# Reordering sixteen matmuls around a late transpose, and dropping four matmuls on zeros, at the start of a 4096 x 4096 matmul with bias and tanh

## Chip, cores, metric

One core of one Trainium2 chip. The metric is device microseconds of one execution. The profile's span (first to last instruction) is about 1.7 us shorter than that.

## The reference

```python
def reference(a, b, bias):          # all 4096 x 4096 float32, bias 4096
    return np.tanh(np.matmul(a, b) + bias)
```

## The kernel before

The product runs in fp16: TensorE multiplies a 128x128 block of A, transposed, by a 128x512 block of B. B is taken in four column chunks of 1024 (J = 2 halves of 512), A in row tiles of 128 rows, and the sum over 4096 runs over 32 k-tiles. One matmul is one row tile, one k-tile, one half.

The first chunk starts before anything is loaded, so it is done in a special order. Groups 0 and 1 of four row tiles each (G = 4) take turns over the k-tiles as they arrive: group 0 over 1 to 4, group 1 over 1 to 8, group 0 over 5 to 16, group 1 over 9 to 32. The part sums of a pass are put aside in SBUF ("spill") and added again later. Eight 128x512 sums (4 row tiles x 2 halves) of a group take all eight PSUM buffers ("banks" below) of the kernel's pool, so a group can only start when sums of the other have been moved out.

```python
def across(ps, ms, t0, t1, first):          # k-tile by k-tile, over the row tiles ms
    for t in range(t0, t1):
        for m in ms:
            for j in range(J):
                mm(ps[m][j], ats[m], b_cur, t, j, t == first, False)

def down(ps, ms, t0, t1, done):             # closes the sums one after the other
    for m in ms:
        for j in range(J):
            for t in range(t0, t1):
                mm(ps[m][j], ats[m], b_cur, t, j, False, t == t1 - 1)
            done(ps[m][j], m, j)            # here add_aside: spill += ps on VectorE

def fill(n, w):                             # n matmuls of w columns on zeros
    ...

# the first row tiles, turned on TensorE, with zeros between them (lines joined here)
turn_nat(0, nc.vector.tensor_copy); fill(3, P); turn_nat(1, nc.scalar.copy)
row(0, 0, 2); fill(2, P); turn_nat(2, nc.vector.tensor_copy)
row(1, 0, 2); fill(2, P); turn_nat(3, nc.scalar.copy)
row(2, 0, 2); row(3, 0, 2)
across(ps, g0, 2, BL - 1, 0)
...
# the order of the loads, all on one queue (KS = 8, KM = 16, BL = TB = 4):
want_a("g0b", G, 0, G * Q, BL, BL)                 # group 0's A, k-tiles 5..8
want_a("g0c", G, 0, G * Q, KS, KM - KS)            # group 0's A, k-tiles 9..16
for u in range(KS, KM, 2):
    want(lambda u=u: load_b_all(u, 2))             # B in pairs, four quarters each
want_a("g1c", ...); want_a("g1d", ...)             # group 1's A, k-tiles 9..16
...                                                # the bias
for t in (KM, KM + 8):
    want_a(("g1", t), G, 4 * P, G * Q, t, 8)
    for u in range(t, t + 8, TB):
        want(lambda u=u: load_b_all(u, TB))        # B four k-tiles at a time
...
# the passage that is reordered
for m in g0:
    turn(ats[m], "g0c", m * Q, KS, KM - KS)        # VectorE transposes
one_by_one(ps, g0, BL, KS, BL)                     # k-tiles 5..8
across(ps, g0, KS, KM - 1, BL)                     # k-tiles 9..15
for i in range(2):
    turn(ats[G + i], "g1c", i * Q, KS, KM - KS)
down(ps, g0, KM - 1, KM, add_aside)                # k-tile 16, frees the banks
...
one_by_one(ps, g1, KS, KM, KS)                     # group 1, k-tiles 9..16
for t in (KM, KM + 8): ...                         # group 1, k-tiles 17..28
```

## Time and profile before

| | |
|---|---|
| device time, 3 runs | 1782.67 us median, 1782.46 to 1783.02 |
| span of the profile | 1780.8 us |
| TensorE | busy 100% of the span, 8258 matmuls |
| its idle time before instructions, whole span | 2.3 us in three waits |

The profile's lines are in the prediction. In a timeline the first two numbers are the start and the length in us, then engine, source line, operation, tiles written and read, and how many instructions were merged; the bracket gives the idle time ahead of them and what ended it. Lengths of matmul groups overlap, so starts are what to compare. The landing of a transfer is its issue time plus the last column of the DMA issues.

### The profile page before, as it was taken

How to read it: one execution, taken by the hardware profiler on the slowest of the kernel's cores; microseconds unless marked ns; L12 is line 12 of the kernel's file. 1: busy time of each engine (PE TensorE's matmuls, PEld its weight loads, DVE VectorE, ACT ScalarE, POOL GpSimd, SP SyncE). 2: the span in 40 equal slices, each digit the busy share in tenths (PEclk: the TensorE clock that was granted, in tenths of full speed). 3: DMA queues.
4: the chain of work that ended last, by engine and by line, in shares of the span. 5: the costliest groups of instructions: out<-in, count | busy, mean ns of one | idle time of the engine just before them, and what ended most of it. 6: DMA issues, size and time to landing. Idle time of an engine off the chain costs nothing.

```text
span 1780.8 us, 20862 instructions
## 1 busy us (share of the span) xinstructions
PE 1775.0 (100%) x8258; PEld 807.1 (45%) x8258; DVE 764.1 (43%) x680; ACT 173.0 (10%) x279; POOL 872.0 (49%) x1618
## 2 busy tenths in 40 slices
PE   9999999999999999999999999999999999999999
PEld 4444444444444444444444444444444444444444
DVE  3764443444334443444334443444344443444342
ACT  2021000000000000000000000000000000000001
POOL 7565566544565554444456554444544454444510
PEclk9999999999999999999999999999999999999999
DMA  9999999976999877767699987766777667766641
GB/s 185 204 194 177 176 167 154 140 125 110 167 173 165 145 112 116 118 116 120 113 170 171 172 136 116 118 116 108 128 116 122 107 113 117 120 114 109 117 77 42
DMA packets 281393, 238.94 MB, mean 134 GB/s; under 512 B 159056, under 2 KB 231760, under 8 KB 281296
## 3 DMA queue, kind: packets, MB, share of 16 engines
q0 software_dynamic: 243280, 167.88, 69.8%
q1 hardware_dynamic: 37728, 69.62, 11.0%
q8 instruction: 64, 1.05, 0.2%
q14 instruction: 33, 0.27, 0.1%
q10 hardware_dynamic: 288, 0.13, 0.0%
HBM read 337.64 MB, written 67.11 MB: 227 GB/s over the span
## 4 chain that ended last, share of the span: by engine, by line
PE 97%; DMA 1%; POOL 0%; DVE 0%; issue 0%; ACT 0%; DVEq 0%; POOLq 0%
PE ps L412 93%; PE ps L138 5%; DMA b<-in_b_dram 1%; DMA an<-in_a_dram 0%; DVE atx L100 0%; POOL an L90 0%; POOL nat L246 0%; POOL b L69 0%; ACT o_sb L152 0%; DVE o_sb L149 0%; POOL ident L263 0%; POOLq L263 0%; DVEq L100 0%; DVEq L149 0%; POOLq L435 0%
## 5 line engine op out<-in xcount | busy, mean ns | idle before, releaser
L412 PE MATMUL ps<-b,at 128*128 128x512 f16 x7712 | 1657.8, 378 | 0.0
L90 POOL DMA_DIRECT2D an<-in_a_dram x1492 | 805.4, 547 | 797.4 <-DVE at L100 592.0
L412 PEld LDWEIGHTS <-at 128*128 128x128 f16 x7712 | 754.6, 98 | 903.3
L100 DVE STREAM_TRANSPOSE at<-an 128x512 f16<-128x512 f16 (+1 forms) x380 | 565.5, 1539 | 65.8 <-DMA an<-in_a_dram 65.8
L149 DVE TENSOR_TENSOR o_sb<-ps,bias_bc 128x512 f32<-128x512 f32 (+1 forms) x243 | 165.7, 683 | 918.4 <-PE ps L412 710.3
L152 ACT ACTIVATE o_sb<-o_sb 128x512 f32<-128x512 f32 (+1 forms) x243 | 151.6, 625 | 1502.3 <-DVE o_sb L149 1502.3
L73 POOL DMA_DIRECT2D b<-in_b_dram x104 | 56.2, 544 | 15.3 <-DMA an<-in_a_dram 7.8
L138 PE MATMUL ps<-b,atx 128*128 128x512 f16 x256 | 56.4, 379 | 0.5 <-DVE atx L100 0.5
L138 PE MATMUL ps<-b,at 128*128 128x512 f16 x256 | 55.6, 379 | 0.0
L138 PEld LDWEIGHTS <-at 128*128 128x128 f16 x256 | 25.0, 98 | 30.2
L138 PEld LDWEIGHTS <-atx 128*128 128x128 f16 x256 | 24.6, 98 | 30.7 <-DVE atx L100 1.8
L100 DVE STREAM_TRANSPOSE atx<-an 128x512 f16<-128x512 f16 (+2 forms) x12 | 16.3, 1399 | 12.3 <-DMA an<-in_a_dram 12.3
L69 POOL DMA_DIRECT2D b<-in_b_dram x12 | 7.8, 654 | 22.5 <-PE ps L412 22.3
L152 ACT ACTIVATE spill<-spill 128x512 f32<-128x512 f32 x16 | 9.9, 630 | 82.9 <-DVE spill L149 82.9
L149 DVE TENSOR_TENSOR spill<-ps,spill 128x512 f32<-128x512 f32 x16 | 10.4, 679 | 10.1 <-PE ps L138 10.1
L181 DVE TENSOR_TENSOR spill<-spill,bias_bc 128x512 f32<-128x512 f32 x16 | 9.7, 677 | 0.0
L173 ACT COPY spill<-ps 128x512 f32<-128x512 f32 x16 | 8.0, 623 | 12.9 <-PE ps L138 12.9
L228 PE MATMUL ps<-zeros 128*128 128x512 f16 (+1 forms) x18 | 5.6, 463 | 1.3 <-DVE zeros L221 1.3
L176 DVE TENSOR_TENSOR spill<-ps,spill 128x512 f32<-128x512 f32 x8 | 4.8, 672 | 0.0
L228 PEld LDWEIGHTS <-zeros 128*128 128x128 f16 x18 | 2.1, 126 | 4.2 <-issue 2.5
L239 DVE CAST b<-spill 128x1024 f16<-128x1024 f32 x1 | 0.9, 871 | 4.5 <-DMA spill<-in_b_dram 4.5
L246 POOL DMA_DIRECT2D nat<-in_a_dram x4 | 2.3, 586 | 0.8 <-POOLq L435 0.8
(14 smaller groups left out, 8.8 us busy)
## 6 DMA issues: line engine op xcount, KB each, us to landing
an<-in_a_dram POOLq DMA_DIRECT2D x480, 192.0 KB, 5.1
out_dram<-o_sb SPq DMA_DIRECT2D x239, 256.0 KB, 2.5
an<-in_a_dram POOLq DMA_DIRECT2D x960, 32.0 KB, 2.6
b<-in_b_dram POOLq DMA_DIRECT2D x94, 256.0 KB, 8.0
b<-in_b_dram POOLq DMA_DIRECT2D x6, 1024.0 KB, 13.2
an<-in_a_dram POOLq DMA_DIRECT2D x32, 128.0 KB, 5.6
out_dram<-spill SPq DMA_DIRECT2D x16, 256.0 KB, 5.6
an<-in_a_dram POOLq DMA_DIRECT2D x12, 256.0 KB, 8.3
```

What stands on the lines that cost most here:

```text
L69: queue.dma_start(out=dst, in_=src[:, ds(t0 % BL, nt), :])
L73: nc.gpsimd.dma_start(out=bt[t0 // TB][ds(q * QP, QP), ds(t0 % TB, nt), :], in_=src.rearrange("(t p) n -> p t n", p=QP),)
L90: nc.gpsimd.dma_start(out=an[ds(q * QP, QP), :, ds((t - t0) * QP, n * QP)], in_=src.rearrange("(mb p) k -> p mb k", p=QP),)
L100: nc.vector.transpose(at[:, ds(t, n), :].rearrange("P t (mb p) -> P mb t p", p=QP), an[:, ds(mb0, Q), ds((t - t0) * QP, n * QP)].rearrange ...
L138: nc.tensor.matmul(ps, at[:, t, :], bt[t // TB][:, t % TB, ts(j, NB)], start=start, stop=stop)
L149: nc.vector.tensor_tensor(out=o_sb[:, piece], in0=ps[:, piece], in1=addend[:, piece], op=mybir.AluOpType.add)
L152: nc.scalar.activation(o_sb[:, piece], o_sb[:, piece], mybir.ActivationFunctionType.Tanh)
L173: nc.scalar.copy(aside(m, j), ps)
L176: nc.vector.tensor_tensor(out=aside(m, j), in0=ps, in1=aside(m, j), op=mybir.AluOpType.add)
L181: nc.vector.tensor_tensor(out=aside(m, j), in0=aside(m, j), in1=bias_bc[:, ts(j, NB)], op=mybir.AluOpType.add)
L228: nc.tensor.matmul(ps[:, ds(0, w)], zeros[:, :P], zeros[:, :w], start=i == 0, stop=i == n - 1)
L412: nc.tensor.matmul(ps, at[:, t, :], b_cur[t // TB][:, t % TB, ds(c0, w)], start=t == 0, stop=t == KT - 1,)
```

## The change

Intent: the k-tiles 9 and 10 were run across all four row tiles, so TensorE stood still until the fourth row tile had been turned. With both k-tiles of a row tile together there are four matmuls to do for each row tile, not two, while the next is being turned. The zeros between the first rows are dropped, as they fill no wait.

```diff
     row(0, 0, 2)
-    fill(2, P)
     turn_nat(2, nc.vector.tensor_copy)
     row(1, 0, 2)
-    fill(2, P)
     turn_nat(3, nc.scalar.copy)
 ...
     one_by_one(ps, g0, BL, KS, BL)
-    across(ps, g0, KS, KM - 1, BL)
+    for m in g0:
+        across(ps, (m,), KS, KS + 2, BL)
+    across(ps, g0, KS + 2, KM - 1, BL)
```

## The prediction

> **What bounds the kernel now.** I read the page first: busy time by engine and the chain that ended last. Then the waits of TensorE over the whole span, then the timelines of TensorE, its weight loads and VectorE over the first 51 us, where both edits lie. These lines are the page's:
>
> ```profile
> PE 1775.0 (100%) x8258; PEld 807.1 (45%) x8258; DVE 764.1 (43%) x680; ACT 173.0 (10%) x279; POOL 872.0 (49%) x1618
> ...
> PE 97%; DMA 1%; POOL 0%; DVE 0%; issue 0%; ACT 0%; DVEq 0%; POOLq 0%
> ```
>
> TensorE is the chain. The count is 8258 matmuls: 8192 for the product, 32 more because the last tile is halved, 16 transposes and 18 matmuls on zeros. Only a matmul that disappears from TensorE's queue, or a wait of TensorE that ends sooner, can move the time. The waits view lists all of TensorE's waits:
>
> ```profile
> PE ps L228 <- DVE zeros L221: 1.3, 1, 1.3
> PE ps L138 <- DVE atx L100: 0.5, 1, 0.5
> PE tp L257 <- DMA nat<-in_a_dram: 0.5, 1, 0.5
> ```
>
> One of them, on a VectorE transpose into atx (group 0's A tiles), concerns the change. Next, TensorE's timeline (start, length, count), with the zeros that go away and then the passage that is reordered:
>
> ```profile
> 7.43 1.04 PE L138 MATMUL ps<-b,atx 128*128 128x512 f16 x4
> 8.31 0.28 PE L228 MATMUL ps<-zeros 128*128 128x128 f16 x2
> 8.42 0.39 PE L257 MATMUL tp<-ident,nat 128*128 128x128 f16 x4
> 8.64 1.03 PE L138 MATMUL ps<-b,atx 128*128 128x512 f16 x4
> 9.51 0.28 PE L228 MATMUL ps<-zeros 128*128 128x128 f16 x2
> 9.62 0.39 PE L257 MATMUL tp<-ident,nat 128*128 128x128 f16 x4
> ```
>
> ```profile
> 28.83 8.54 PE L138 MATMUL ps<-b,atx 128*128 128x512 f16 x38
> 37.90 12.69 PE L138 MATMUL ps<-b,atx 128*128 128x512 f16 x58 [0.52 <-DVE atx L100]
> 50.42 41.60 PE L138 MATMUL ps<-b,at 128*128 128x512 f16 x192
> ```
>
> Use the starts, not the lengths, because the ends overlap. From 37.90 to 50.42 there are 58 matmuls, so one takes 0.216 us. By that pace the 38 matmuls from 28.83 would be through at 28.83 + 38 x 0.2158 = 37.03; the next starts at 37.90. So 0.87 us is lost in that stretch, more than the 0.52 that the waits view shows. The weight loads show where:
>
> ```profile
> 35.79 0.56 PEld L138 LDWEIGHTS <-atx 128*128 128x128 f16 x4 [0.38 <-DVE atx L100]
> 36.76 0.11 PEld L138 LDWEIGHTS <-atx 128*128 128x128 f16 x2 [0.41 <-DVE atx L100]
> 37.89 0.55 PEld L138 LDWEIGHTS <-atx 128*128 128x128 f16 x4 [1.01 <-DVE atx L100]
> ```
>
> The load at 35.79 opens the ninth k-tile (32 matmuls after 28.83, due at 35.74); those at 36.76 and 37.89 open its third and fourth row tile. What released each is in VectorE's timeline and in the DMA issues:
>
> ```profile
> 33.22 4.62 DVE L100 STREAM_TRANSPOSE atx<-an 128x1024 f16<-128x1024 f16 x4 [2.89 <-DMA an<-in_a_dram]
> 47.43 2.37 DVE L100 STREAM_TRANSPOSE at<-an 128x1024 f16<-128x1024 f16 x2 [9.59 <-DMA an<-in_a_dram]
> 49.72 2.44 DVE L176 TENSOR_TENSOR spill<-ps,spill 128x512 f32<-128x512 f32 x4
> ```
>
> ```profile
> 28.03 0.54 POOL L73 DMA_DIRECT2D b<-in_b_dram  x1 [0.23 <-DMA an<-in_a_dram]
> ```
>
> ```profile
> b<-in_b_dram POOLq DMA_DIRECT2D x1, 128.0 KB, 7.7
> ```
>
> Four transposes from 33.22 to 37.84, one per row tile, end some 1.13 apart: about 34.46, 35.59, 36.71 and 37.84. The last two match the loads at 36.76 and 37.89. The first stall is different: the releaser view names VectorE, but row tile 0 was turned at 34.46. The last quarter of B's ninth and tenth k-tile, issued at 28.03, landed 7.7 us later, at 35.73. That is the event the load at 35.79 follows. So the 0.87 us is about 0.08 waiting for B and 0.77 waiting for transposes, with 0.02 of pipeline restart.
>
> **What the Trainium skill says.** "TensorE: Matmul & The Clock Gate", section "Wait — 56ns, not 53.3ns?", gives 55.6 and 215.7 ns between warm matmuls of 128 and 512 columns. The trace agrees: two zero matmuls take 8.31 to 8.42, 55 ns each, and a 512-column one 216 ns. The same page, Part 1, has the clock fall after an idle window of about 3.4 us; the trace's longest stall past the warm-up is about 0.7 us and the granted clock stays full, so a moved stall of that size should not cost speed. "PSUM — Partial Sum Buffer", section "The four PSUM rules", says one matmul output takes at most one bank; its specifications list eight banks. This kernel's eight open 128x512 sums of group 0 therefore fill PSUM: group 1's first sum waits for a freed bank. The same page, "Engine vs sequencer instructions", says VectorE's queue is strict FIFO. The trace agrees: the add that empties the first bank starts at 49.72, behind the two transposes that started at 47.43, although the sum it reads ended near 49.08 (matmul start 48.70 plus 0.38).
>
> **The change part by part.**
>
> 1. *Zeros removed.* Four 128-column matmuls at 55.8 ns: TensorE gets 0.22 us ahead from 8.31 on. The transposes that follow need A tiles already loaded (they ran at once, with no wait, in the trace). Each copy of a transposed tile moves with its transpose, and the distance from transpose to the row that uses it is unchanged or is still ample. VectorE's turn of row tile 0 for k-tiles five to eight, which began at 27.83 and takes about 0.71, ends at 28.54, while the shifted matmul is due at 28.61: it just holds.
>
> 2. *But at the ninth k-tile* TensorE now arrives at 35.74 - 0.22 = 35.52, and B still lands at 35.73. Transfers do not depend on TensorE here: their buffers come free through VectorE's transposes, which wait for transfers. So the first matmul stays at 35.82 and the 0.22 is gone.
>
> 3. *Two k-tiles per row tile.* From 35.82 each row tile has 4 matmuls, 0.863 us, in place of 2. Row tile 1 is due at 36.68 (turned 35.59), 2 at 37.55 (36.71), 3 at 38.41 (37.84). The smallest reserve is 0.57. B's tenth k-tile comes in the same transfers as the ninth. The 16 matmuls end at 35.82 + 16 x 0.2158 = 39.27, where before they ended at 37.90 + 10 x 0.2158 = 40.06. Gain: 0.79 us. The three later B pairs are issued from 29.34 on and land 5.3 us later in the median, the first of them complete at 38.20: over a microsecond of reserve.
>
> 4. *What follows.* After k-tiles 11 to 15, the eight closing matmuls shift from 48.70 to 47.91 and TensorE is ready for group 1 at 49.63 in place of 50.42. Its first sum needs the bank of group 0's first sum. VectorE's order is unchanged: two transposes, from 47.43 because their A transfer landed just then, then the add. The transposes hold it until 49.72; the add takes 0.65, so the bank is free at 50.37, and with the 0.05 us that the earlier releases took (37.84 to 37.89) TensorE starts at 50.42. That is exactly where it starts now: in this trace the two paths, the late transposes through 58 matmuls and the transfer through VectorE, meet within 0.01 us. The change shortens one of them.
>
> Sum: 0.22 + 0.79 gained on TensorE, 0.22 given back at 35.8, 0.79 at 50.4. Net 0.0 us. After 50.42 TensorE has no wait to the end, so nothing is gained or lost there.
>
> **The rivals.** (a) *The gain passes through*: time falls by 0.79 to 1781.9. For it: the waits view shows no wait at 50.42. Against it: only because both paths tie; the add's start at 49.72 does not involve TensorE. (b) *The zeros' 0.22 counts also*: 1781.66. Against it: B's landing at 35.73. (c) *The tie was chance*: the transfers of single executions jitter, and in some the transposes' path was the later one, so the change saves the excess. The three times before differ by 0.56 us, so I allow 0.1 us on average. (d) *Slower*: with two zero tiles fewer, PSUM banks are handed out in another order, and a row might wait for a copy. All copies but the last row tile's are done well before, and that row needs its copy anyway: under 0.2 us, 1782.8. (e) *A clock effect* from the missing zeros: transposes take only 0.22 us between rows, so I expect none.
>
> **Range and chances.** From the median 1782.67, with 0.0 by the working and 0.1 for (c): 1782.6. The low end, 1781.8, takes in rival (a) with a little scatter; the high end, 1783.1, is the slowest run before plus 0.1. Two per cent is 36 us, while all of TensorE's waits sum to 2.3 us: within 2% is 0.99, faster 0.004, slower 0.006.
>
> **What would show it right or wrong.** Right: TensorE has 8254 matmuls; no wait on atx; the ninth k-tile still opens at about 35.8 and the weight load's idle time there grows from 0.38 to 0.60; a new TensorE wait appears on the add into spill, of about 0.6 (0.79 less the modelled overlap of 0.16), ending near 50.4; group 1's passage starts within 0.1 of 50.42. Wrong: that passage starting near 49.6, which would mean the bank came free earlier, or VectorE's add not behind the transposes; or the ninth k-tile opening at 35.6, which would mean B is not what holds it. A wait later than 50.4 would also refute it.

## The result

The first four runs of the changed kernel took 1781.87 us in the median (1781.57 to 1782.08), beside 1782.85 for the four of before (1782.46 to 1784.16). The ratio is 0.9993, with an interval of 0.9976 to 1.001. Ratios here are the mean time of one kernel's runs over that of the other's in the same rounds, so not quite the ratio of the medians. The kernel won about 0.8 us by its median against the 1782.67 foretold from, where the prediction had the net at nothing and allowed 0.1.

Single executions scatter with a standard deviation of 0.55 us, so I pool. Over all, before has 45 runs with a mean of 1782.72 us and the changed kernel 14 with 1782.20: 0.52 us less, with a standard error of 0.16 (the root of the sum of the two squared errors). These pools cross chips. They also show that the first four runs were lucky: a gain of 0.52 us on 1782.67 would be 1782.15.

The page of the changed kernel, busy times and the chain:

```profile
PE 1774.4 (100%) x8254; PEld 806.9 (45%) x8254; DVE 763.8 (43%) x680; ACT 173.2 (10%) x279; POOL 872.1 (49%) x1618
...
PE 99%; DMA 0%; issue 0%; ACT 0%; POOL 0%; DVE 0%; DVEq 0%; POOLq 0%
```

Four matmuls fewer, as they should be. TensorE's timeline of the changed kernel:

```profile
8.31 0.39 PE L257 MATMUL tp<-ident,nat 128*128 128x128 f16 x4
...
28.70 21.10 PE L138 MATMUL ps<-b,atx 128*128 128x512 f16 x96
49.63 41.84 PE L138 MATMUL ps<-b,at 128*128 128x512 f16 x192
```

The transpose now follows the row at 8.31, where the zeros stood. All 96 matmuls of group 0 run in one piece, where they were broken at 37.90. Group 1's passage opens at 49.63, not at 50.42: the 0.79 us of step 3 to the hundredth, and no wait on the bank. This is a sign that the prediction had named for being wrong.

The weight loads of the changed kernel, at the ninth and at the 25th k-tile, and VectorE behind group 1's opening:

```profile
35.79 13.51 PEld L138 LDWEIGHTS <-atx 128*128 128x128 f16 x64 [0.51 <-DVE atx L100]
```

```profile
76.83 0.10 PEld L138 LDWEIGHTS <-at 128*128 128x128 f16 x1
77.47 0.13 PEld L138 LDWEIGHTS <-at 128*128 128x128 f16 x2 [0.55 <-DVE spill L181]
```

```profile
46.16 2.37 DVE L100 STREAM_TRANSPOSE at<-an 128x1024 f16<-128x1024 f16 x2 [8.22 <-DMA an<-in_a_dram]
48.46 4.84 DVE L176 TENSOR_TENSOR spill<-ps,spill 128x512 f32<-128x512 f32 x8
```

The ninth k-tile opens at 35.8, as before, after a longer idle time (0.51 for 0.38; 0.60 was predicted). VectorE began its transposes for group 1 at 46.16, not at 47.43, because A's transfer landed sooner; so the add that frees the first bank was done at 49.11, before TensorE came. And there is a new stall: the 25th k-tile opens at 77.50 (the load at 77.47), 0.24 late.

That stall is not in TensorE's waits view, since the modelled end of the matmul before it covers most of it, and the weight loads' view names a bias add on VectorE that had ended at 77.01. The DMA issue of the last quarter of B's k-tiles 25 to 28 tells more. First the issue and its landing time in the changed kernel, then the same in the kernel before:

```profile
66.62 0.55 POOL L73 DMA_DIRECT2D b<-in_b_dram  x1 [0.68 <-DMA b<-in_b_dram]
```

```profile
b<-in_b_dram POOLq DMA_DIRECT2D x1, 256.0 KB, 10.6
```

```profile
67.52 0.55 POOL L73 DMA_DIRECT2D b<-in_b_dram  x1 [0.71 <-DMA b<-in_b_dram]
```

```profile
b<-in_b_dram POOLq DMA_DIRECT2D x1, 256.0 KB, 10.1
```

It landed at 77.26 in the changed kernel and 77.60 in the one before (unrounded). TensorE opened the 25th k-tile at 77.50 and 78.05. "Perfetto Trace Analysis", section "Identifying Dependency Chains", says that an instruction that waits for several engines may have extra semaphore instructions ahead of it. The trace has two here, one behind the other, and with them the 0.24 us from landing to opening; in all four profiles that stall there, the lag is 0.24 or 0.25. So before the change, B held the 25th k-tile to 77.84 at the earliest, and TensorE came 0.21 later. After it, TensorE would have come at 77.26 and B held it. Of the 0.79, 0.55 is left at 77.50, and the spans differ by just that, 1780.8 and 1780.2. From the opening of the 25th k-tile to the end of the span it is 1702.72 us in both, and 1702.71 to 1702.73 in all 17 profiles: what is not won by then is not won at all.

### The profile page after: what moved, and what is told of

Its sections match the earlier page's. It is cut to its first block, busy times and chain, and to the rows that moved or that the text cites. A ratio compares the mean times of both kernels' runs of the same rounds, so it can differ in the third digit from the quotient of the medians.

```text
span 1780.2 us, 20854 instructions
## 1 busy us (share of the span) xinstructions
PE 1774.4 (100%) x8254; PEld 806.9 (45%) x8254; DVE 763.8 (43%) x680; ACT 173.2 (10%) x279; POOL 872.1 (49%) x1618
## 4 chain that ended last, share of the span: by engine, by line
PE 99%; DMA 0%; issue 0%; ACT 0%; POOL 0%; DVE 0%; DVEq 0%; POOLq 0%
PE ps L412 93%; PE ps L138 6%; DMA nat<-in_a_dram 0%; ACT o_sb L152 0%; PE tp L257 0%; POOL nat L246 0%; DVE o_sb L149 0%; DVEq L149 0%; POOLq L435 0%
```

## The experiments

For every profile I read the same four openings. Without a stall, group 1 opens 48 matmuls (10.36 us at 0.2158) after group 0's eleventh k-tile, and the 25th k-tile 128 matmuls (27.62 us) after that. What exceeds these is the wait at group 1's bank and the wait for B:

| kernel | 9th opens | 11th | group 1 | 25th | bank wait | B wait | VectorE starts group 1's transposes | B's last quarter lands |
|---|---|---|---|---|---|---|---|---|
| before | 35.82 | 40.06 | 50.42 | 78.05 | 0 | 0 | 47.43 | 77.60 |
| before, again | 35.95 | 40.03 | 50.39 | 78.02 | 0 | 0 | 46.77 | 77.70 |
| zeros out only | 35.83 | 40.16 | 50.52 | 78.14 | 0 | 0 | 46.74 | 77.79 |
| reordering only | 35.84 | 39.28 | 49.65 | 78.21 | 0 | 0.94 | 46.35 | 77.97 |
| changed | 35.82 | 39.27 | 49.63 | 77.50 | 0 | 0.24 | 46.16 | 77.26 |
| changed, again | 36.77 | 40.22 | 50.60 | 79.02 | 0.02 | 0.79 | 47.60 | 78.77 |
| changed, third | 35.84 | 39.29 | 50.03 | 77.65 | 0.38 | 0 | 47.03 | 77.20 |

My first theory (T1) was that the reordering's 0.79 us passes through because the tie at 50.42 was chance, and that the zeros bring nothing. The rivals were that the zeros carry a share (R1) and my prediction (R2).

### Zeros out only

The two `fill(2, P)` are removed and the old `across` stays.

> Only the four zero matmuls are taken out; the ninth and tenth k-tile stay as before. Theory T1 (the gain is the reordering's; the time won by the zeros is lost again where B's ninth k-tile lands at 35.8 us): time as before, within 0.2 us; group 1's passage starts near 50.4 us. Rival R1 (the zeros carry a share): 0.2 us faster than before. Rival R2 (my prediction: the bank that group 1 needs comes free no sooner than TensorE arrives): as before.

Time: 1782.57 us median, ratio 0.9999 (0.9986 to 1.0011). The weight load that opens the ninth k-tile:

```profile
35.80 0.56 PEld L138 LDWEIGHTS <-atx 128*128 128x128 f16 x4 [0.55 <-DVE atx L100]
```

The ninth k-tile opens as before, after a longer idle time (0.55 for 0.38). In this profile R1 is out: the zeros' 0.22 us ends at B's landing, as step 2 had it. The times cannot tell 0 from 0.2.

### Reordering only

The zeros stay; the passage is that of the change.

> Only the reordering of the ninth and tenth k-tile; the zero matmuls stay. T1: as the whole change, 0.5 to 0.8 us faster than before; group 1's passage starts at 49.6 us with no wait on the add into spill in most profiles. R1: 0.2 us slower than the whole change. R2: the passage starts when the bank is free, as late as 50.4 if A's transfer for group 1 lands at 47.3 as it did before.

Time: 1782.66 us median, 1781.91 to 1784.29; ratio 1.0 (0.9988 to 1.0013). The expected 0.5 to 0.8 us did not show. TensorE's timeline of this kernel:

```profile
49.65 27.79 PE L138 MATMUL ps<-b,at 128*128 128x512 f16 x128
78.21 2.10 PE L138 MATMUL ps<-b,at 128*128 128x512 f16 x9 [0.78 <-DMA b<-in_b_dram]
```

Group 1 opens as early as with the whole change, and then the 25th k-tile waits for B: 0.94 us, more than all that was won. Here the waits view names the transfer itself. T1 is only half right: the bank does let the gain through, and another place takes it.

### Before and changed, a second time

Both unedited.

> The kernel before, unchanged, for a second profile and for the noise. T1: A's transfer for group 1 lands about a microsecond sooner than the 47.3 us of the first profile, so that the tie at 50.42 us was chance; time ratio 1.000 within 0.0002. R2: it lands at 47.3 again and the tie is there again.

> The changed kernel, unchanged, for a second profile. T1: group 1's passage starts at 49.6 us, A's transfer for it lands near 46 us, and the wait of some 0.2 us for B's 25th k-tile at 77.5 us is there again, so that the time is 0.5 to 0.8 us below before. R2: a profile of this kernel in which that transfer lands at 47.3 us shows a wait on the add into spill of up to 0.6 us and a start at 50.4 us.

Before: ratio 0.9999, no tie: VectorE's transposes began at 46.77, 0.66 sooner than in the first profile, while TensorE opened group 1 at 50.39:

```profile
46.77 2.37 DVE L100 STREAM_TRANSPOSE at<-an 128x1024 f16<-128x1024 f16 x2 [8.96 <-DMA an<-in_a_dram]
```

Changed: median 1782.15, ratio 0.9996 (0.9982 to 1.001); its profiled run happened to be the slowest of its five, 1783.46. TensorE's timeline in it:

```profile
29.64 21.10 PE L138 MATMUL ps<-b,atx 128*128 128x512 f16 x96 [0.61 <-ACT spill L173]
50.60 27.79 PE L138 MATMUL ps<-b,at 128*128 128x512 f16 x128
79.02 13.32 PE L138 MATMUL ps<-b,at 128*128 128x512 f16 x61 [0.63 <-DVE spill L181]
```

The whole start is late by 0.95: VectorE's turn for k-tiles 5 to 8 began at 28.87, not at 27.93, behind a later transfer, and the later landings are late too. The releaser that the view names at 29.64 and at 79.02 is not the cause in either place. That led to my second theory, T3: TensorE follows the transfers from 29 us to 79 us, and what it wins between two of them it gives back at the next. It does not hold at every opening: in the second profile of before, B's ninth k-tile landed at 35.61, 0.34 before TensorE opened it. The DMA row of the kernel before, 25 to 50 us in 40 slices, shows the DMA engines busy 90% or more in all slices but one, so the transfers run nearly without a pause:

```profile
DMA  9999999999999999999989999999999999999999
```

### Finer load of B's 25th k-tile, with and without the change

```diff
-        for u in range(t, t + 8, TB):
-            want(lambda u=u: load_b_all(u, TB))
+        for u, nt in ((t, TB), (t + TB, TB)) if t == KM else ((t, 2), (t + 2, 2), (t + TB, TB)):
+            want(lambda u=u, nt=nt: load_b_all(u, nt))
```

> The changed kernel with B's k-tiles 25 to 28 loaded as two pairs in place of four at once, so that the 25th and 26th land some 2.5 us sooner. Theory T3 (what the change won by 49.6 us is partly lost where TensorE opens the 25th k-tile, because B's last quarter for it lands there; the transfers of the first 80 us set that moment): no stall at the 25th k-tile, which opens 27.6 us after group 1's passage started (64 matmuls to the 17th, 64 to the 25th, at 0.2158 us); of the order of 0.2 to 0.9 us faster than the changed kernel, with a smaller spread of the times. Rival R3 (the stall at the 25th k-tile is VectorE's, which the waits view names: its transposes of A or its bias adds): the stall stays and the time is that of the changed kernel.

> The kernel before with the same finer load. T3: before the change TensorE reached the 25th k-tile just after B did, so little is gained: 0 to 0.3 us, and the whole change on top of it is then worth 0.8 us in the opening of the 25th k-tile. R3: as before, and the change is worth no more than without the finer load.

With the change: 1781.93 us median, ratio 0.9996 (0.9983 to 1.001), and the passage of group 1 through the 25th k-tile in one piece:

```profile
49.66 41.60 PE L138 MATMUL ps<-b,at 128*128 128x512 f16 x192
```

B now lands at 74.83, and the 25th k-tile opens at 77.29, 27.63 after the passage began. R3 is out: nothing on VectorE was edited, and the stall is gone in this profile and in the four later ones that have the new order and the finer load. The 0.2 to 0.9 us over the changed kernel, which I expected, did not show in the times (the pools at the end say 0.12 +- 0.18). Without the change: 1782.89, ratio 1.0 (0.9987 to 1.0012), opening at 78.45 because the ninth had opened 0.3 late, at 36.14. The finer load alone is worth nothing, as T3 has it. The expected smaller spread did not come (1781.74 to 1782.86).

### Two useless transposes ahead of the adds

Group 1's second row tile is turned twice more, which holds VectorE 2.25 us longer before the add that frees the first bank. Results stay right.

```diff
+    g1c_an = staged["g1c"][0]
     for i in range(2):
         turn(ats[G + i], "g1c", i * Q, KS, KM - KS)
+        if i == 0:
+            for _ in range(2):
+                transpose_a(ats[G + 1], g1c_an, Q, KS, KM - KS)
```

> The changed kernel with group 1's second row tile turned twice more than needed (2.25 us of VectorE) ahead of the adds that free group 0's banks. This makes the wait that my prediction expected. If the bank path works as predicted and only its time was wrong, TensorE waits 1.5 to 1.9 us at the opening of group 1's passage, released by the add into spill; the 25th k-tile then opens without a stall at 79.0 to 79.4 us and the time is 0.9 to 1.5 us above the changed kernel's. If the bank is not what group 1 waits for, no wait and no change.

> The kernel before with the same two useless turns. If the bank path had a reserve of some 0.6 us in most executions (T1), group 1's passage starts 1.4 to 1.7 us late and the change is worth nothing on top: the passage opens within some tenths of the same moment as in the changed kernel with these turns, the rest being the jitter of the transfers. If the tie of the first profile were the rule (R2), it starts 2.25 us late, at 52.7 us.

One run each: 1783.68 and 1784.54 us. TensorE's timeline with the change, then without:

```profile
51.62 40.74 PE L138 MATMUL ps<-b,at 128*128 128x512 f16 x188 [1.79 <-DVE spill L176]
```

```profile
52.49 39.87 PE L138 MATMUL ps<-b,at 128*128 128x512 f16 x184 [1.05 <-DVE spill L176]
```

So the mechanism that I predicted is real: delay the add, and group 1 waits for it, 1.95 us start to start with the change and 1.22 without. The opening is 5.56 us after VectorE's first transpose in both (46.06 and 46.93). The two openings are 0.87 apart, more than the tenths expected, because the transfers were. With the change the 25th k-tile opened at 79.25 without a stall, as expected. The waits are a little outside what I had written (1.5 to 1.9 and 1.4 to 1.7).

### Group 0's A in two halves around B's ninth k-tile

On top of the finer load, with the zeros out, and then with the zeros put back (the turns of row tiles 3 and 4 then read `g0c2`, not shown):

```diff
-    want_a("g0c", G, 0, G * Q, KS, KM - KS)
-    for u in range(KS, KM, 2):
+    want_a("g0c", 2, 0, 2 * Q, KS, KM - KS)
+    want(lambda: load_b_all(KS, 2))
+    want_a("g0c2", 2, 2 * P, 2 * Q, KS, KM - KS)
+    for u in range(KS + 2, KM, 2):
         want(lambda u=u: load_b_all(u, 2))
```

> The changed kernel with two edits of the order of its loads: B's 25th and 26th k-tile ahead of the 27th and 28th (as in the earlier run), and group 0's A for k-tiles 9 to 16 loaded in two halves, two row tiles before B's ninth and tenth k-tile and two after. T3: B's ninth k-tile then lands near 33 us and the stall at its opening (0.21 us in three profiles of four with the change) is gone; no stall at the 25th. The 25th k-tile opens 0.2 to 0.3 us sooner than with the finer load alone, near 77.05 us when the transfers before 28 us are not late; 0.7 to 1.1 us faster than before. Rival: the split only moves the stall to a transpose of the third or fourth row tile, or to later pairs of B, and nothing is won over the finer load alone.

> The same with the four zero matmuls put back. T3: with B's ninth k-tile no longer holding TensorE, the zeros show for the first time: the ninth k-tile opens 0.1 to 0.22 us later than without them, unless the transposes for k-tiles 5 to 8 hold TensorE at 28.7 us in that run, in which case nothing shows. Rival: no difference in any case, as TensorE waits for something else.

1782.25 us median, 1782.18 to 1782.50, ratio 0.9998 (0.9984 to 1.0011); and one look at 1782.17 with the zeros. B's ninth k-tile lands at 33.20 and the stall at its opening is gone (35.69 without zeros, 35.88 with them: 0.19, within the 0.1 to 0.22 that the zeros were expected to show). But the rival came true. Without the zeros 0.19 us is lost at the fourth row tile of the ninth k-tile, whose A now comes in the later half. Its transpose, the second of the two from 36.04, ended at 38.41, and its weight load follows at 38.47:

```profile
36.04 2.37 DVE L100 STREAM_TRANSPOSE atx<-an 128x1024 f16<-128x1024 f16 x2 [2.89 <-DMA an<-in_a_dram]
38.47 2.06 PEld L138 LDWEIGHTS <-atx 128*128 128x128 f16 x11 [0.52 <-DVE atx L100]
```

B's eleventh k-tile, which also landed at 38.47, was needed only at 39.35. With the zeros, where the ninth opened later, nothing is lost there, and both have the same start of the 11th k-tile to 0.02 us (39.35 and 39.33). Then the bank binds, by 0.46 us without the zeros and 0.42 with them. TensorE without them:

```profile
50.16 41.60 PE L138 MATMUL ps<-b,at 128*128 128x512 f16 x192 [0.29 <-DVE spill L176]
```

The 25th opens at 77.79 without zeros and 77.73 with them. The split wins nothing in its profiles, and the finer load alone does not guarantee the gain: the bank can take it. Its five times lie closest together of all, which I have not followed up.

### Changed, a third time; finer load, a second time

> The changed kernel a third time, beside the others on one chip. T3: 0.3 to 0.9 us faster than before, with a stall of 0.2 to 0.8 us at the 25th k-tile that ends about 0.24 us after the last quarter of B lands.

> The changed kernel with the finer load of B's 25th k-tile, a second time. T3: no stall at the 25th k-tile, which opens 27.6 us after group 1's passage; between the changed kernel and the one with both edits in time, within the scatter of some 0.4 us of each mean.

Changed: 1782.57 us median, ratio 0.9998 (0.9985 to 1.001), and, against the expectation, no stall at the 25th but the bank wait that I had predicted. TensorE and VectorE in it:

```profile
50.03 41.60 PE L138 MATMUL ps<-b,at 128*128 128x512 f16 x192 [0.22 <-DVE spill L176]
```

```profile
47.03 2.37 DVE L100 STREAM_TRANSPOSE at<-an 128x1024 f16<-128x1024 f16 x2 [9.09 <-DMA an<-in_a_dram]
```

The bank comes free 3.00 us after the transposes start: 47.03 to 50.03 here, 47.60 to 50.60 in the second profile, 47.43 to 50.42 in the first of before. It binds where this sum is later than TensorE. Finer load: 1782.05, ratio 0.9997 (0.9984 to 1.0009); transfers late at the ninth (36.54), group 1 at 50.35, the 25th at 77.97, no wait for the bank or for B. The transposes began at 47.35 here, so the bank came free at 50.35 too: a tie once more.

### Both gates opened

There are thus two gates, places where TensorE may have to wait: the bank at group 1's opening and B at the 25th k-tile. The finer load opens the second. The first opens with the adds of row tile 0 put ahead of the second turn on VectorE:

```diff
-    for i in range(2):
-        turn(ats[G + i], "g1c", i * Q, KS, KM - KS)
-    down(ps, g0, KM - 1, KM, add_aside)
+    turn(ats[G], "g1c", 0, KS, KM - KS)
+    down(ps, (0,), KM - 1, KM, add_aside)
+    turn(ats[G + 1], "g1c", Q, KS, KM - KS)
+    down(ps, (1, 2, 3), KM - 1, KM, add_aside)
```

> The changed kernel with one edit: on VectorE the first two adds into spill stand ahead of the turn of group 1's second row tile, so that the first bank comes free 1.1 us sooner. If the queue on VectorE is what holds the bank, group 1's passage opens without a wait, 10.36 us after the eleventh k-tile (48 matmuls at 0.2158 us), even when A's transfer for it is late (transposes from 47 us on). The gate at B's 25th k-tile stays: a stall of 0.2 to 0.9 us there. Time within 0.3 us of the changed kernel's, 0.3 to 0.8 us below before.

> The changed kernel with both gates open: the adds ahead of the second turn, and B's 25th and 26th k-tile loaded first. If the two gates are the whole cause, TensorE has no stall after the ninth k-tile opens and the 25th opens 37.98 us after the eleventh (176 matmuls at 0.2158 us), near 77.3 us; 0.7 to 1.0 us faster than before in the mean. If a third gate exists, a stall appears elsewhere.

> The kernel before with both gates open. If the gates are the whole cause, this is worth 0 to 0.2 us: the 0.6 to 0.7 us wait for the fourth row tile's transpose stays, and the 25th k-tile opens near 78.0 us, 0.7 to 0.8 us later than with the change and the gates open. If opening the gates is itself the gain, this kernel is as fast as the changed one with the gates open.

The bank's gate alone, on the changed kernel: 1783.08 us median (1781.87 to 1783.34), ratio 1.0001 (0.9988 to 1.0013), worse than I expected in time; in the profile group 1 opens on time, at 49.34, and the 25th k-tile waits 0.48 for B:

```profile
77.44 13.97 PE L138 MATMUL ps<-b,at 128*128 128x512 f16 x64 [0.32 <-DMA b<-in_b_dram]
```

In this execution VectorE began at 46.73, so the bank would have been free at 49.73 in the old order, 0.39 after TensorE came. So here the old order on VectorE would have held it. (TensorE lost 0.05 us at the eleventh k-tile as well, where B came late in this execution, at 38.84.)

Both gates, with the change: 1781.97 us median, ratio 0.9996 (0.9983 to 1.001). Both gates, without: 1782.71, ratio 1.0 (0.9988 to 1.0013). The means of the two are 0.63 apart. TensorE with the change, then without:

```profile
29.21 21.07 PE L138 MATMUL ps<-b,atx 128*128 128x512 f16 x96
50.11 41.60 PE L138 MATMUL ps<-b,at 128*128 128x512 f16 x192
```

```profile
37.51 12.69 PE L138 MATMUL ps<-b,atx 128*128 128x512 f16 x58 [0.25 <-DVE atx L100]
50.04 41.60 PE L138 MATMUL ps<-b,at 128*128 128x512 f16 x192
```

The single profiles miss the absolute times that I expected: the 25th opens at 77.74 with the change and at 77.66 without, as the ninth opened at 36.30 in the first and 35.80 in the second. Counted from the ninth, the stretch to the 25th is 41.44 with the change, which is 192 matmuls at 0.2158 us with no loss at all, and 41.87 without. VectorE's transposes began at 47.33 with the change, so in the old order of the adds the bank would have been free at 50.33, 0.22 after TensorE came: the earlier add was needed in this execution. Without the change 0.42 us is lost at the fourth row tile's transpose, a little less than the 0.6 to 0.7 expected. No third gate showed. That opening the gates is itself the gain is out: without the change it brings nothing (0.06 us slower than before in the mean).

Counted so, the stretch from ninth to 25th:

| | profiles | from the 9th to the 25th, us |
|---|---|---|
| old order (before twice, zeros out, finer load, both gates) | 5 | 41.87 to 42.31, mean 42.16 |
| new order, B's gate as it was (changed three times, reordering only, adds first) | 5 | 41.68 to 42.38, mean 42.02 |
| new order, B's gate open (finer load twice, both gates) | 3 | 41.44 in each |

The table leaves out the two kernels with useless transposes and the two with A in halves (42.09 and 41.85, where the bank bound).

In time, the three sets of runs of the last row have a mean of 1782.08 us over 15 runs and those with the same loads in the old order (finer load, both gates) 1782.70 over 10: 0.61 less, standard error 0.19. Against all runs of before it is 0.64 +- 0.14. Every single run's own interval includes 1; the gain rests on these pools and on the profiles. The kernel with the change and both gates open is the one that I would keep. That the kernels of the last row beat the changed kernel (1782.08 to 1782.20, 0.12 +- 0.18) shows in the profiles and not in the times.

## Why the prediction was wrong

**What bounds it** held: TensorE's queue, and the time from the opening of the 25th k-tile to the end of the span is 1702.72 us before and after.

**Steps 1 and 2** (the zeros) held. The turn for k-tiles 5 to 8 that "just holds" did not quite: the matmul due at 28.61 started at 28.70, 0.09 later, which B's wait at the ninth k-tile swallowed along with the rest; so the idle time there grew to 0.51 and not to 0.60. The zeros can count where B is earlier: 0.19 us with A in halves. And in the run with the adds first, B's ninth k-tile landed at 35.36 and TensorE, with the zeros out, opened it at 35.47 without a wait.

**Step 3** held: 39.27 was predicted for the end of the two k-tiles, and 39.27 to 39.31 were measured in the five profiles of the new order where the ninth opened between 35.82 and 35.86. The stretch of 16 matmuls takes 3.45 us in nine of the eleven profiles of the new order (3.51 and 3.65 in the two that had a stall in it), against 3.88 to 4.33 in those of the old order. Its "over a microsecond of reserve" for B's eleventh k-tile was once more a single execution's: with the adds first B landed only 0.14 us before TensorE opened that k-tile, 0.05 late.

**Step 4** failed. "The transposes hold it until 49.72" took the landing of one transfer in one execution for a property of the kernel. In the 15 profiles that load group 0's A in one piece the transposes start anywhere from 46.06 to 47.60, with a median of 46.74; 47.43, from which I worked, is the second latest. Three microseconds later the bank is free. So the tie "within 0.01 us", on which the whole sum rested, was chance. The mechanism is real (it bound in the third profile by 0.38 us, with A in halves by 0.46 and 0.42, and by 1.95 when provoked), but not in force in most profiles of the new order, and my weight for rival (c), 0.1 us, was far too small.

**"After 50.42 TensorE has no wait to the end, so nothing is gained or lost there"** failed too. No wait before the change does not mean a reserve. I gave a reserve for B up to the eleventh k-tile and none for the loads behind it. At the 25th it was 0.21, 0.08 and 0.11 us in three profiles with the old order and the old loads (the opening less the landing of B plus 0.24), far less than 0.79. So a second place, which I never looked at, takes part of the gain: 0.24, 0.79, 0.94 and 0.48 us in four of five profiles. Rival (a), that it all passes through, is therefore not what happened either; the full gain of the stretch stayed only in profiles with B's load made finer, and of those only where the bank did not bind.

The median, 1781.87, lies at the very edge of the range (1781.8 to 1783.1), with one of its four runs below; scaled by the ratio of the same rounds, 1782.67 x 0.9993 = 1781.4, it is outside. Chance has a part in that, as the pooled gain of 0.52 us is smaller than that of the first four runs. In all these readings the centre was wrong by its claim that the net is nothing.

**What stays open**: how the loss is shared between the two gates in the mean. Three profiles of the changed kernel lose 0.24, 0.81 and 0.38 us of 0.79, a mean of 0.48, which would leave 0.3; the times say 0.52 +- 0.16. The two do not contradict each other, given the scatter, but neither fixes the share. The reordering without the zeros' removal and the kernel with the adds first leave B's gate as it was, too, and their runs are not faster than before (0.08 slower and 0.02 faster than the pool); with them, the new order with B's old load is 0.29 +- 0.16 us faster over 24 runs. So how much of the change arrives without the finer load is not settled by the times. What makes a transfer land up to 1.5 us sooner or later in one execution than in another is open as well.

## What to carry to other kernels

A path that shows no wait may have a reserve of nothing: before counting a gain on TensorE, take every later point where it meets a transfer or a freed buffer, and subtract landing plus lag from arrival there, up to the end of the stretch that is fed from memory. Where two paths meet within hundredths in one profile, ask for a second profile before building on which of them is later. And when a small gain vanishes, look for the next transfer that arrives just in time; loading the first needed part of it in a smaller piece can be what lets the gain through.

## What the Trainium skill lacked or had wrong

- No page that I read says how far a transfer's landing moves between executions of one kernel. Here the same transfer released VectorE at 46.06 to 47.60 us in 15 profiles, and the last quarter of B's 25th k-tile landed at 77.03 to 78.77 in the ten with unchanged loads for it.
- "Perfetto Trace Analysis", section "Identifying Dependency Chains", names the extra semaphore instructions of a wait for several engines, but no cost. Here the matmul started 0.24 us after the last of four quarters had landed at the 25th k-tile, 0.09 us at the ninth, and 0.05 us after a release with a single source.
- "TensorE: Matmul & The Clock Gate", section "Back-to-back issue gap", gives a sustained 131 ns for a 512-column matmul in a stream with weight loads. Every undisturbed stream here, with one weight load for each matmul, runs at 215.8 ns; the section calls about 216 ns the gap of an isolated matmul only.
